# Layer A's attention: value products gathered into two runs per unit, far part of the older unit first

## The chip, the cores and the metric

The kernel runs on one core of one Trainium2 chip. The metric is the device time of one execution in microseconds, median of several runs. A core has five engines that run side by side, each through its own queue of instructions in order: TensorE (PE, matmuls, with its weight loads as PEld), VectorE (DVE), ScalarE (ACT), GpSimd (POOL) and SyncE (SP, which only issues DMAs here). They wait for each other by semaphores. Matmuls write to PSUM; the other engines move results from there to SBUF.

## The reference

A decoder trunk of two layers over 1024 tokens of width 1024 in float32. Layer A is a sparse attention of 16 heads in 4 groups, with three branches that a sigmoid gate weighs (scores on compressed blocks of keys; 8 chosen of 16 blocks of 64 keys for each query and group; the last 256 keys), and a SwiGLU. Layer B attends over shared keys in three dilations. The change is in layer A's attention:

```
def nsa_attention(h, w_in, b_gate, ...):
    ...
    p, denom, _ = masked_softmax(s + bias_c, dist_c >= 0)
    p_cmp = p / jnp.maximum(denom, 1e-30)
    o_cmp = jnp.einsum('bgrsn,bngd->bsgrd', p_cmp, v_cmp.astype(jnp.float32))
    ...
    _, sel_idx = lax.top_k(score, top_n)
    ...
        p_sel, den, _ = masked_softmax(s_sel, (dist >= 0)[:, :, :, None, :])
        return jnp.einsum('bcgrk,bgckd->bcgrd', p_sel / jnp.maximum(den, 1e-30), vg.astype(jnp.float32))
    ...
    o_win, _ = banded_attention(q, kvh(kwn), kvh(vwn), WIN - 1, 1, rel_bias)
    g = jax.nn.sigmoid((gl + b_gate).astype(jnp.float32)).reshape(B, S, N_KV, GQA_R, 3)
    o = g[..., 0:1] * o_cmp + g[..., 1:2] * o_sel + g[..., 2:3] * o_win
```

## The kernel before

Layer A's attention goes over 32 units: for each of 4 groups of heads (g) 8 tiles of 128 queries (t). A unit has 4 heads. All its weights, already divided by their sums and multiplied by the gate, lie in SBUF with the queries on the partitions, so they must be turned (transposed) before they can be multiplied with the values.

A unit's steps, as letters of the table `steps`: `a` and `b` are near scores (L821; the keys of the last 256 tokens in blocks t-2 to t, together with the 63 compressed blocks) of heads 0, 1 and 2, 3; `c` are the weights of the compressed blocks and, for t of 4 and more, the choice of key blocks; `m` turns that choice into rows of the queries (L876); `f` and `g` are far scores (L908, L909; the selected branch over all t + 1 blocks of keys) of the two pairs of heads; `n` are near values, `v` far values (both L436). A score tile `s` in PSUM (4 buffers) is read by a reduction on DVE (L822, L824, L910) that adds the bias and finds the extreme; then come ACT (L801, exponentials with sums), DVE (L803, reciprocals) and POOL (L805, scaling).

For values, `turned` (L367) takes one block of 128 keys: four transposes on PE (L371) into a PSUM tile `pt` (3 buffers), and one copy (L378) into an SBUF tile `pT` (5 buffers), in turn on ACT and DVE. `values` (L417) makes parts of up to three blocks: the transposes of a part, and then its products with the values (L436). A block's products are two matmuls of 64 columns each, for the heads of the upper and the lower half of the output; the float32 matmul appears as two records each in the profile, so a block has four. Near values have one part, of 1 to 3 blocks and the turned compressed weights (`vc`); far values have one part for 1 to 3 blocks, two for 4 to 6 and three for 7 and 8. Near and far of a unit add up in the same half of the PSUM tile `o`, near first; two units in turn use the two halves. A copy on DVE (L923) takes the finished half to `oT`.

`turn(i)` (L958) records the steps of neighbouring units in one order: near scores `a` of unit i+2; `m` and `f` of unit i; far values `v` of unit i-1; `b` and `c` of unit i+2; `n` and `g` of unit i. Loads for later units are issued at a turn's head by SyncE, the near keys (`load_kw`) three units ahead. The written order is not the last word: a scheduler places the instructions of each engine when the program is built, within their dependences and the `after` marks, which keep an instruction behind another.

Of the kernel before, what the change touches and what calls it, by code (L numbers as in the profile page):

```python
# [129 lines left out]
def trunk(ctx, tc, I, out):  # L130
# [85 lines left out]
    def after(prev):  # L216
        return tc.issue_after(prev.ins) if prev is not None else ExitStack()
# [173 lines left out]
    copies, pt_bufs = [0], [5]  # L391
# [25 lines left out]
    def values(p, po, Ps, vs, first, last, behind=None, more=None):  # L417

        nb = len(vs)
        ends = [nb * (i + 1) // -(-nb // 3) for i in range(-(-nb // 3))]
        for lo, hi in zip([0] + ends, ends):
            ts = []
            for b in range(lo, hi):
                copies[0] += 1
                t, prev = turned(p, [Ps[hp][:, e, b * 128:(b + 1) * 128] for e in range(2) for hp in range(2)],
                                 (nc.scalar.copy, nc.vector.tensor_copy)[copies[0] % 2])
                ts.append(t)
            ops = [(vs[b], vs[b], ts[b - lo][:, :256], ts[b - lo][:, 256:]) for b in reversed(range(lo, hi))]  # L430
            if more is not None and lo == 0:
                ops.append(more)
            for i, (*v, ta, tb) in enumerate(ops):
                with after(prev), after(behind if lo == i == 0 else None):
                    for e, t in enumerate((ta, tb)):
                        mm = nc.tensor.matmul(po[64 * e:64 * e + 64, :256], v[e], t, start=first and lo == i == 0,  # L436
                                              stop=last and hi == nb and i == len(ops) - 1, skip_group_check=True)
                prev = mm
        return prev
# [34 lines left out]
    with ExitStack() as c:  # L474
# [332 lines left out]
        def near_scores(g, t, hp):  # L807
# [8 lines left out]
            for e in range(2):  # L816
# [3 lines left out]
                for z in range(2):  # L820
                    nc.tensor.matmul(ps[:, :w], q, K[z][:, :w], start=z == 0, stop=z == 1)  # L821
# [58 lines left out]
        def near_values(g, t):  # L880
            pc = blocks_[g, t][0]
            pT, _ = turned(wk, [pc[:, 2 * c:2 * c + 2, :] for c in range(2)], nc.vector.tensor_copy)
            po = po_[g, t] = outs()
            k0 = max(t - 2, 0)
            ends[0] = values(wk, po, grp["P2", g, t], [grp["V", 1, g, b // 4][:, b % 4, :] for b in range(k0, t + 1)],
                             True, False, ends[0], (vc[:, g, :64], vc[:, g, 64:], pT[:, :256], pT[:, :256]))

        def far_scores(g, t, hp):
# [10 lines left out]
            for e in range(2):  # L899
                hh = 2 * hp + e  # L900
                q = query(g, t, hh)
                for i, (lo, hi, a) in enumerate(cuts):
# [6 lines left out]
                    nc.tensor.matmul(ps[:, :max(rw, 256)], ql[:nr], kl[:nr, ks], start=False, stop=True)  # L909
# [9 lines left out]
        def far_values(g, t):  # L919
            po = po_[g, t]  # L920
            ends[0] = values(wk, po, grp["P1", g, t], [grp["V", 0, g, b // 4][:, b % 4, :] for b in range(t + 1)],
                             False, True)
            nc.vector.tensor_copy(oT[:, 2 * g:2 * g + 2, tok(t)], po.rearrange("p (c q) -> p c q", q=128))  # L923
# [50 lines left out]
    with ExitStack() as c:  # L974
# [10 lines left out]
        outs, ends = Turns([o_[:, :256], o_[:, 256:]]), [None]  # L985
        for i in range(0, len(units) + 1):
            turn(i)
    kctx.close()
# [1137 lines left out]
```

## Time and profile before

| | us |
|---|---|
| median of 3 runs | 2747.96 (2747.43 to 2748.98) |
| the profiled execution | 2750.92 |
| its span, first to last instruction | 2749.1 |
| layer A's attention, first to last value product | 283.3 to 671.8 |
| mean granted TensorE clock, share of full | 0.999 |

In the answers of the profile, a row names an instruction by its line, engine, operation and its tiles, output first (`o<-pT,V`: value products of turned weights with far values; `VW` are near values, `vc` the compressed ones). `L436` is line 436 of the kernel before. For a matmul, the first size is that of the stationary operand, the second that of the moving one (128\*64 and 128x256: a contraction over 128 keys, 64 columns of the array, 256 columns of queries). The ends of matmuls are modelled and overlap, so the distance between two starts tells more about TensorE than the busy time.

### The profile page before, as it was taken

How to read it: one execution, taken by the hardware profiler on the slowest of the kernel's cores; microseconds unless marked ns; L12 is line 12 of the kernel's file. 1: busy time of each engine (PE TensorE's matmuls, PEld its weight loads, DVE VectorE, ACT ScalarE, POOL GpSimd, SP SyncE). 2: the span in 40 equal slices, each digit the busy share in tenths (PEclk: the TensorE clock that was granted, in tenths of full speed). 3: DMA queues.
4: the chain of work that ended last, by engine and by line, in shares of the span. 5: the costliest groups of instructions: out<-in, count | busy, mean ns of one | idle time of the engine just before them, and what ended most of it. 6: DMA issues, size and time to landing. Idle time of an engine off the chain costs nothing.

```text
span 2749.1 us, 42939 instructions
## 1 busy us (share of the span) xinstructions
PE 2714.2 (99%) x14448; PEld 2212.3 (80%) x14448; DVE 2211.1 (80%) x4532; ACT 1409.9 (51%) x3165; POOL 1372.5 (50%) x1446
## 2 busy tenths in 40 slices
PE   9999999999999999999999999999999999999999
PEld 8988676776888888888878888888878888888887
DVE  5443888986988989898885677688899888898888
ACT  5531777775653334344454544577766433343435
POOL 3135655552356656556356787411103755656562
PEclk9999999999999999999999999999999999999999
DMA  5678743223122232222223555697441212112112
GB/s 173 188 235 299 202 126 107 63 74 143 54 73 62 73 82 66 69 58 74 65 89 115 144 149 172 208 268 237 113 176 45 75 56 60 50 52 64 54 54 77
DMA packets 291900, 312.24 MB, mean 114 GB/s; under 512 B 50300, under 2 KB 229165, under 8 KB 291680
## 3 DMA queue, kind: packets, MB, share of 16 engines
q1 hardware_dynamic: 271280, 247.30, 30.6%
q0 software_dynamic: 20400, 62.20, 7.3%
q8 instruction: 114, 1.87, 0.3%
q14 instruction: 106, 0.87, 0.1%
HBM read 241.99 MB, written 81.04 MB: 118 GB/s over the span
## 4 chain that ended last, share of the span: by engine, by line
PE 88%; DVE 5%; DMA 3%; ACT 1%; SPq 1%; issue 1%; POOL 0%; ACTq 0%; DVEq 0%; POOLq 0%
PE ux L1241 19%; PE uy L1241 16%; PE dx L1052 8%; PE pt L371 6%; PE dr L1052 6%; PE dr L1241 5%; PE o L436 4%; PE mm L239 3%; PE mm L240 3%; PE mm L241 3%; PE o L412 2%; PE dx L1241 2%; PE s L821 1%; DVE pl L1011 1%; PE s L909 1%; PE dx L239 1%
## 5 line engine op out<-in xcount | busy, mean ns | idle before, releaser
L1011 DVE TENSOR_TENSOR pl<-oT,ph 128x512 fp32r<-128x512 f32 x336 | 343.4, 1040 | 74.1 <-PE ux L1241 19.5
L1010 ACT ACTIVATE ph<-oT 128x512 fp32r<-128x512 f32 x342 | 209.7, 627 | 232.7 <-PE ux L1241 54.6
L371 PE MATMUL pt<-ident,P 128*128 128x128 f32 x1536 | 232.2, 278 | 2.9 <-ACT pT L378 1.3
L1011 DVE TENSOR_TENSOR pl<-oTb,ph 128x512 fp32r<-128x512 f32 x228 | 207.9, 935 | 24.0 <-PE dr L1052 17.2
L1010 ACT ACTIVATE ph<-oTb 128x512 fp32r<-128x512 f32 x234 | 142.6, 626 | 161.8 <-PE ux L1241 53.4
L1446 POOL TENSOR_TENSOR oT<-oT,gffn 128x512 f32<-128x512 f32 x92 | 115.7, 1268 | 216.9 <-DMA oT<-in_ffn_w_up_dram 92.6
L371 PEld LDWEIGHTS pt<-ident,P 128*128 128x128 f32 x1536 | 174.9, 141 | 59.9 <-issue 42.9
L805 POOL TENSOR_SCALAR P<-P,sm,gates 128x384 f32<-128x384 f32 (+7 forms) x256 | 182.1, 722 | 81.6 <-DVE sm L803 57.6
L1057 DVE TENSOR_TENSOR xrfx<-xrfx,dr 128x512 f32<-128x512 f32 x320 | 204.0, 678 | 13.6 <-PE dr L1052 13.6
L1057 DVE TENSOR_TENSOR xrfx<-xrfx,dx 128x512 f32<-128x512 f32 x320 | 204.0, 676 | 0.9 <-PE dx L1052 0.9
L801 ACT ACTIVATE P<-P,m 128x384 f32<-128x384 f32 (+7 forms) x256 | 170.6, 668 | 35.6 <-DVE m L914 13.9
L1446 POOL TENSOR_TENSOR oTb<-oTb,gffn 128x512 f32<-128x512 f32 x92 | 107.6, 1179 | 161.0 <-DMA oTb<-in_ffn_w_up_dram 98.5
L378 DVE COPY pT<-pt 128x512 f32<-128x512 f32 (+1 forms) x208 | 131.6, 644 | 36.8 <-PE pt L371 30.8
L378 ACT COPY pT<-pt 128x512 f32<-128x512 f32 x176 | 100.4, 576 | 102.9 <-PE pt L371 102.4
L1932 ACT ACTIVATE P<-P,st 128x384 f32<-128x384 f32 (+2 forms) x256 | 139.4, 547 | 24.4 <-DVE st L1927 24.1
L1927 DVE CUSTOM_DVE_ANT_0 P<-s,T 128x384 f32<-128x384 f32 (+2 forms) x256 | 110.2, 475 | 6.6 <-PE s L1957 1.6
L1052 PE MATMUL dx<-ph,pl 128*128 128x512 f32 x320 | 107.2, 390 | 0.5 <-DVE pl L1011 0.5
L1052 PE MATMUL dx<-ph 128*128 128x512 f32 x320 | 107.3, 389 | 0.0
L910 DVE CUSTOM_DVE_ANT_0 P<-s,T 128x128 f32<-128x128 f32 (+3 forms) x192 | 99.2, 549 | 7.2 <-PE s L909 6.9
L239 PE MATMUL mm<-hH,wh 128*128 128x512 f32 (+1 forms) x272 | 102.8, 379 | 0.0
L240 PE MATMUL mm<-hL,wh 128*128 128x512 f32 (+1 forms) x272 | 102.6, 379 | 0.0
L241 PE MATMUL mm<-hH,wl 128*128 128x512 f32 (+1 forms) x272 | 102.3, 377 | 0.0
(649 smaller groups left out, 8028.5 us busy)
## 6 DMA issues: line engine op xcount, KB each, us to landing
qB<-xrfx POOLq DMA_DIRECT2D x96, 256.0 KB, 5.1
oT<-in_ffn_w_up_dram SPq DMA_DIRECT2D x92, 256.0 KB, 2.9
oTb<-in_ffn_w_up_dram SPq DMA_DIRECT2D x92, 256.0 KB, 2.9
Q<-qB SPq DMA_DIRECT2D x40, 512.0 KB, 6.9
wd<-in_ffn_w_down_dram SPq DMA_DIRECT2D x60, 256.0 KB, 2.6
oT<-in_b_w_q_dram SPq DMA_DIRECT2D x48, 256.0 KB, 3.5
wraw<-in_a_w_in_dram SPq DMA_DIRECT2D x18, 512.0 KB, 5.7
KW<-kS SPq DMA_DIRECT2D x96, 96.0 KB, 2.7
```

Of the source, the lines that this page charges most:

```text
L239: nc.tensor.matmul(ps, lh, rh, start=first, stop=False, skip_group_check=bool(shared))
L240: nc.tensor.matmul(ps, lh, rl, start=False, stop=False, skip_group_check=bool(shared))
L241: return nc.tensor.matmul(ps, ll, rh, start=False, stop=last, skip_group_check=bool(shared))
L371: prev = nc.tensor.transpose(ps[:, i * 128:(i + 1) * 128], h, ident)
L378: copy(t[:, :w], ps[:, :w])
L805: nc.gpsimd.tensor_scalar(P[:, e, :n], P[:, e, :n], sm[:, e:e + 1], gate(e), op0=OP.mult, op1=OP.mult)
L1010: self.high = nc.scalar.activation(h, src, AF.Copy)
L1011: self.last = (eng or nc.vector).tensor_sub(l, src, f32(h))
L1052: nc.tensor.matmul(banks[t], part(a, t)[u], b[v], start=z == 0 and onX != 2, stop=z == 2, skip_group_check=True)
L1057: nc.vector.tensor_add(xs, xs, banks[t])
L1241: mm = nc.tensor.matmul(b, x[:, i * 128:(i + 1) * 128], ys[i], start=first and (z, i) == (0, 0), stop=(z, i) == (2, 3), skip_group_check=True)
L1446: nc.gpsimd.tensor_mul(v, v, gains[:, k:k + 4].unsqueeze(2).to_broadcast([128, 4, 128]))
```

## The change

The value products are no longer made at the end of each part. `values` is replaced by `values_parts`, which only turns the blocks of a part, holds them in a list (`held`) and returns one function per part, and `held_values`, which makes the products of all that is held in one run. Within a run the far part of the older unit, whose half of `o` is already opened, comes first, with the part turned last ahead; then the near part of the newer unit opens the other half. Each run is kept behind the last run, behind the last transposes that were held, and behind the last score matmul recorded (`scored`).

In `turn(i)`, units of three far parts (t of 6 and 7) have a first run in mid-turn with their first two parts. The remaining far part or parts of unit i-1 are turned behind the near blocks of unit i, and both have one run at the turn's end. Units with two far parts have the first of them turned in mid-turn, and held. Scores stand between the turned parts: `m` and `f` of unit i first, the first far part of unit i-1, then `a` of unit i+2, the second far part (where there are three), and `b`, `c`, `g`. The copy of a finished half to `oT` is recorded with the next part that is turned, not at once. There are 12 `pT` buffers instead of 5, and the program sets the space for POOL's DMA descriptors to 4096 bytes of a partition.

```diff
-    copies, pt_bufs = [0], [5]
+    copies, pt_bufs = [0], [12]
...
-    def values(p, po, Ps, vs, first, last, behind=None, more=None):
...
+    held, opened, ended, outputs, scored = [], set(), [None], [], [None]
+
+    def values_parts(p, po, Ps, vs, more=None, done=None):
+
+        def part(lo, hi):
+            ops = [more()] if more is not None and lo == 0 else []
             for b in range(lo, hi):
                 copies[0] += 1
                 t, prev = turned(p, [Ps[hp][:, e, b * 128:(b + 1) * 128] for e in range(2) for hp in range(2)],
                                  (nc.scalar.copy, nc.vector.tensor_copy)[copies[0] % 2])
...
+                ops.append((vs[b], vs[b], t[:, :256], t[:, 256:]))
+            held.append((po, ops, done if hi == len(vs) else None, prev))
+            while outputs:
+                outputs.pop(0)()
...
+    def held_values():
+
+        prev = held[-1][3]
+        run = [h for h in reversed(held) if id(h[0]) in opened] + [h for h in held if id(h[0]) not in opened]
+        over = [id(h[0]) for h in run if h[2] is not None]
+        last = {id(h[0]): k for k, h in enumerate(run)}
+        for k, (po, ops, done, _) in enumerate(run):
+            u = id(po)
+            for i, (*v, ta, tb) in enumerate(reversed(ops)):
+                with after(prev), after(ended[0]), after(scored[0]):
                     for e, t in enumerate((ta, tb)):
...
+                opened.add(u)
                 prev = mm
...
+        ended[0] = prev
+        held.clear()
...
-            for what, d in [('a', 2), ('m', 0), ('f', 0), ('v', -1), ('b', 2), ('c', 2), ('n', 0), ('g', 0)]:
-                if 0 <= i + d < len(units):
-                    steps[what](units[i + d])
+            far = steps['v'](units[i - 1]) if i > 0 else []
...
+            some([('m', 0), ('f', 0)])
+            if len(far) == 3:
+                far.pop(0)()
+            some([('a', 2)])
+            if len(far) == 2:
+                far.pop(0)()
+                if len(held) == 2:
+                    held_values()
+            some([('b', 2), ('c', 2), ('g', 0)])
+            for part in (steps['n'](units[i]) if 0 <= i < len(units) else []) + far:
+                part()
+            if held:
+                held_values()
...
-    nc = bacc.Bacc("TRN2", target_bir_lowering=False, num_devices=1)
+    nc = bacc.Bacc("TRN2", target_bir_lowering=False, num_devices=1, dynamic_dma_scratch_size=4096)
```

What the scheduler made of it, in TensorE's order, at unit (1, 4), whose turn ends with the near values of its own blocks 2, 3 and 4 (`VW`, two tiles) and has the far values of unit (1, 3), four blocks (`V`). Before, the first part of the far values:

```order
L909 MATMUL s<-K_3014,QM_4332 128x512
L436 MATMUL o<-pT,V_3019 64x256 x2
L371 MATMUL pt<-ident,P_4871 128x128
L371 MATMUL pt<-ident,P_4992 128x128
L371 MATMUL pt<-ident,P_4871 128x128
L371 MATMUL pt<-ident,P_4992 128x128
L436 MATMUL o<-pT,V_3019 64x256 x2
L371 MATMUL pt<-ident,pc_2527 128x128 x2
```

and some 20 rows later, before too, the second part and then the near values:

```order
L371 MATMUL pt<-ident,P_4750 128x128
L436 MATMUL o<-pT,V_3019 64x256 x4
L876 MATMUL pt<-ident,mk 16x128
L908 MATMUL s<-K_3013,Q_4324 128x256
L908 MATMUL s<-K_3013,Q_4324 128x512
L371 MATMUL pt<-ident,P_5047 128x128
L908 MATMUL s<-K_3013,Q_4326 128x256
L908 MATMUL s<-K_3013,Q_4326 128x512
L371 MATMUL pt<-ident,P_5047 128x128
L436 MATMUL o<-pT,VW_4334 64x256 x2
L436 MATMUL o<-pT,VW_3912 64x256 x4
L436 MATMUL o<-pT,vc 64x256 x2
```

In the changed order the same products, at the end of the turn:

```order
L371 MATMUL pt<-ident,P_4929 128x128
L893 MATMUL pt<-ident,mk 16x128
L929 MATMUL s<-K_3013,Q_4323 128x256
L929 MATMUL s<-K_3013,Q_4323 128x512
L929 MATMUL s<-K_3013,Q_4325 128x256
L929 MATMUL s<-K_3013,Q_4325 128x512
L447 MATMUL o<-pT,V_3019 64x256 x2
L371 MATMUL pt<-ident,P_5026 128x128
L447 MATMUL o<-pT,V_3019 64x256 x6
L447 MATMUL o<-pT,VW_4333 64x256 x2
L447 MATMUL o<-pT,VW_3911 64x256 x4
L447 MATMUL o<-pT,vc 64x256 x2
```

Products that stood in four places stand in two, with one transpose of the next unit between them; the score matmuls that parted the far and the near products now stand ahead of all of them. In the whole stage the products have 107 places before and 48 after.

On VectorE, the copy of the finished half to `oT`. Before (the output is that of unit (1, 3)), behind a copy of a turned block:

```order
L378 COPY pT<-pt 128x512
L851 TENSOR_TENSOR dg<-cd,gates 128x4
L923 COPY oT<-o 128x2x128
L859 TENSOR_REDUCE a_5140<-pn 128x55
L803 RECIPROCAL sm<-sm 128x2
```

and in the changed order:

```order
L880 TENSOR_TENSOR sc<-sc,a_5117 128x16
L881 TENSOR_TENSOR sc<-sc,force 128x16
L883 MAX m_5124<-sc 128x8
L944 COPY oT<-o 128x2x128
L885 MATCH_REPLACE s_5126<-m_5124,sc 128x16
L931 ISA P_5223,mp<-s,T_4335 128x256
```

The copy moved behind the sums over the compressed weights (`a`, `sc`), which stood behind it before, and ahead of the reductions of the next unit's far scores.

More of the change, by code (lines that the diff above doesn't have):

```diff
@@ L428, in values @@
                                  (nc.scalar.copy, nc.vector.tensor_copy)[copies[0] % 2])
[L429 to L434, printed above, removed]
+                ops.append((vs[b], vs[b], t[:, :256], t[:, 256:]))
+            held.append((po, ops, done if hi == len(vs) else None, prev))
+            while outputs:
+                outputs.pop(0)()
+        nb = len(vs)
+        ends = [nb * (i + 1) // -(-nb // 3) for i in range(-(-nb // 3))]
+        return [lambda lo=lo, hi=hi: part(lo, hi) for lo, hi in zip([0] + ends, ends)]
+    def held_values():
[7 more added lines that the diff above has]
+                with after(prev), after(ended[0]), after(scored[0]):
                     for e, t in enumerate((ta, tb)):
-                        mm = nc.tensor.matmul(po[64 * e:64 * e + 64, :256], v[e], t, start=first and lo == i == 0,
-                                              stop=last and hi == nb and i == len(ops) - 1, skip_group_check=True)
+                        mm = nc.tensor.matmul(po[64 * e:64 * e + 64, :256], v[e], t, start=u not in opened,
+                                              stop=u in over and last[u] == k and i == len(ops) - 1,
+                                              skip_group_check=True)
+                opened.add(u)
                 prev = mm
-        return prev
+            if u in over and last[u] == k:
+                opened.discard(u)
+                outputs.extend(h[2] for h in run if h[0] is po and h[2])
+        ended[0] = prev
+        held.clear()
     def pipelined(jobs, lag=1):
@@ L820, in near_scores @@
                 for z in range(2):
[L821 removed]
+                    scored[0] = nc.tensor.matmul(ps[:, :w], q, K[z][:, :w], start=z == 0, stop=z == 1)
                 nc.vector.tensor_tensor_reduce(out=P[:, e, :n], in0=ps[:, DH:DH + n], in1=grp["TW", g, hh][:, 384 - n:],
@@ L881, in near_values, with blocks @@
             pc = blocks_[g, t][0]
-            pT, _ = turned(wk, [pc[:, 2 * c:2 * c + 2, :] for c in range(2)], nc.vector.tensor_copy)
+            def blocks():
+                pT, _ = turned(wk, [pc[:, 2 * c:2 * c + 2, :] for c in range(2)], nc.vector.tensor_copy)
+                return vc[:, g, :64], vc[:, g, 64:], pT[:, :256], pT[:, :256]
             po = po_[g, t] = outs()
             k0 = max(t - 2, 0)
-            ends[0] = values(wk, po, grp["P2", g, t], [grp["V", 1, g, b // 4][:, b % 4, :] for b in range(k0, t + 1)],
-                             True, False, ends[0], (vc[:, g, :64], vc[:, g, 64:], pT[:, :256], pT[:, :256]))
+            return values_parts(wk, po, grp["P2", g, t], [grp["V", 1, g, b // 4][:, b % 4, :] for b in range(k0, t + 1)],
+                                blocks)
         def far_scores(g, t, hp):
@@ L920, in far_values, with done @@
             po = po_[g, t]
-            ends[0] = values(wk, po, grp["P1", g, t], [grp["V", 0, g, b // 4][:, b % 4, :] for b in range(t + 1)],
-                             False, True)
-            nc.vector.tensor_copy(oT[:, 2 * g:2 * g + 2, tok(t)], po.rearrange("p (c q) -> p c q", q=128))
+            def done():
+                nc.vector.tensor_copy(oT[:, 2 * g:2 * g + 2, tok(t)], po.rearrange("p (c q) -> p c q", q=128))
+            return values_parts(wk, po, grp["P1", g, t], [grp["V", 0, g, b // 4][:, b % 4, :] for b in range(t + 1)],
+                                None, done)
         def loads(g, t):
@@ L961, in turn, with some @@
                 load_kw(i + 3)
-            for what, d in [('a', 2), ('m', 0), ('f', 0), ('v', -1), ('b', 2), ('c', 2), ('n', 0), ('g', 0)]:
-                if 0 <= i + d < len(units):
-                    steps[what](units[i + d])
+            far = steps['v'](units[i - 1]) if i > 0 else []
+            def some(order):
+                for what, d in order:
+                    if 0 <= i + d < len(units):
+                        steps[what](units[i + d])
+            some([('m', 0), ('f', 0)])
[11 more added lines that the diff above has]
+                held_values()
         proj_q(6)
@@ L984, in trunk @@
         o_ = psum["o"].tile([128, 512], F32, name="o", bufs=1)
-        outs, ends = Turns([o_[:, :256], o_[:, 256:]]), [None]
+        outs = Turns([o_[:, :256], o_[:, 256:]])
         for i in range(0, len(units) + 1):
             turn(i)
+        for f in outputs:
+            f()
     kctx.close()
```

6 lines of the change are left out of this document (1 added, 5 removed).

## The prediction, made before the changed kernel ran

> **What bounds the kernel now.** I read the page first, for the busy engine, then the stage of layer A's attention by windows, then what TensorE waits for there, and last single rows in order of time.
>
> ```profile
> PE 2714.2 (99%) x14448; PEld 2212.3 (80%) x14448; DVE 2211.1 (80%) x4532; ACT 1409.9 (51%) x3165; POOL 1372.5 (50%) x1446
> ...
> PE 88%; DVE 5%; DMA 3%; ACT 1%; SPq 1%; issue 1%; POOL 0%; ACTq 0%; DVEq 0%; POOLq 0%
> ```
>
> TensorE (PE) is busy 99% of the span and makes up 88% of the chain that ended last. The change touches one stage only; its value products begin at 283.3 us and end at 671.8 us:
>
> ```profile
> L436 PE MATMUL o<-pT,V x576: 379/379/431, 292.5 to 671.3; 128*64 128x256 f32 x192
> L436 PE MATMUL o<-pT,VW x336: 379/379/431, 283.3 to 661.8; 128*64 128x256 f32 x168
> L436 PE MATMUL o<-pT,vc x128: 379/379/379, 283.8 to 662.2; 128*64 128x256 f32 x128
> ```
>
> These 1040 records are 260 blocks of 128 keys, four records each. The stage by stretches (columns: stretch, its length, busy time of PE, PEld, DVE, ACT, POOL with counts, granted clock, DMA share and GB/s): the ramp of the first units, then the rest of group 0, and groups 1 to 3.
>
> ```profile
> 276.00:316.30 40.30, 35.13 (x204) 24.91 (x203) 31.76 (x168) 31.08 (x119) 29.78 (x64) 0.96 0.85 222
> ...
> 316.30:389.10 72.80, 71.45 (x514) 51.66 (x515) 60.15 (x264) 50.89 (x152) 39.08 (x70) 1.00 0.58 152
> 389.10:486.30 97.20, 95.95 (x672) 68.38 (x671) 80.75 (x367) 71.58 (x227) 56.05 (x101) 1.00 0.36 101
> 486.30:581.60 95.30, 93.99 (x668) 68.12 (x666) 80.28 (x368) 70.52 (x224) 53.20 (x92) 1.00 0.30 84
> 581.60:671.80 90.20, 87.18 (x620) 61.59 (x618) 69.18 (x281) 60.28 (x168) 42.44 (x63) 1.00 0.21 71
> ```
>
> After the ramp PE is busy 97 to 99% and VectorE (DVE) 77 to 84%. What PE waited for from 316.3 us on, in total, times and longest:
>
> ```profile
> PE o L436 <- ACT pT L378: 2.8, 6, 0.7
> PE pt L371 <- ACT pT L378: 1.3, 3, 0.5
> PE o L436 <- DVE pT L378: 0.9, 4, 0.3
> PE pt L371 <- DVE pT L378: 0.6, 2, 0.3
> ```
>
> These four are all but 0.2 us of it: 5.6 us in 355. So PE sets the pace, and what counts is how densely its instructions start. The busy share hides this, since matmuls overlap; starts show it (columns: start, length, then the instruction):
>
> ```profile
> 364.80 0.40 PE L909 MATMUL s<-K,QM 80*128 80x512 f32 x1
> 365.04 0.60 PE L371 MATMUL pt<-ident,P 128*128 128x128 f32 x4
> 365.57 1.08 PE L436 MATMUL o<-pT,V 128*64 128x256 f32 x8
> 366.58 1.10 PE L371 MATMUL pt<-ident,P 128*128 128x128 f32 x8
> ...
> 370.39 0.66 PE L371 MATMUL pt<-ident,P 128*128 128x128 f32 x4
> 370.88 0.38 PE L371 MATMUL pt<-ident,pc 128*128 128x128 f32 x2
> 371.02 0.36 PE L908 MATMUL s<-K,Q 128*128 128x256 f32 x1
> ...
> 477.56 0.65 PE L436 MATMUL o<-pT,V 128*64 128x256 f32 x4
> 478.14 0.66 PE L371 MATMUL pt<-ident,P 128*128 128x128 f32 x4
> ...
> 481.01 1.51 PE L436 MATMUL o<-pT,V 128*64 128x256 f32 x12
> 482.45 0.66 PE L371 MATMUL pt<-ident,P 128*128 128x128 f32 x4
> ...
> 656.43 0.38 PE L371 MATMUL pt<-ident,pc 128*128 128x128 f32 x2
> 656.65 0.60 PE L371 MATMUL pt<-ident,P 128*128 128x128 f32 x4
> ```
>
> **What a change between value products and other work costs.** Two transposes in a row start 0.22 us apart from what follows (656.43 to 656.65), so one is 0.11. One block of products takes 477.56 to 478.14, 0.58 us until the next transpose; three blocks take 481.01 to 482.45, 1.44. Two more blocks cost 0.86, so a block is 0.43 and leaving a run of products costs 0.58 - 0.43 = 0.15 us. The four transposes behind a run take 0.49 (370.39 to 370.88) where four are 0.44: 0.05 more. The four ahead of a run take 0.53 (365.04 to 365.57): 0.09 more. Together **0.30 us for each run of value products**, whatever its length. The value products use half the array's columns (128*64 in the rows) and everything around them all of them (128*128); whatever the cause, the price hangs on the changeover, and no wait is shown at these rows.
>
> **The change part by part.**
>
> *Fewer runs.* In the stage's order before, the products stand in 107 runs; as written they would be 92 (32 of near keys, 60 of far keys), and the scheduler cut some. In the changed order they stand in 48: one at the end of each of 33 turns, one more for each of the 8 units with 7 or 8 far blocks, and 7 cuts by the scheduler. Matmuls, transposes, copies and DMAs stay the same in number on every engine. 59 runs fewer x 0.30 = **17.7 us off PE's path**, if PE still sets the pace.
>
> *The ramp.* In the first 40.3 us PE is busy for only 35.1; it waits on others, and its longest waits are these:
>
> ```profile
> PE s L821 <- DVE cm L824: 1.2, 2, 0.8
> PE s L821 <- DVE sc L864: 1.2, 1, 1.2
> PE s L821 <- DMA KW<-kS: 0.6, 1, 0.6
> ```
>
> Six runs become three there; 3 x 0.30 = 0.9 us saved beside waits are worth nothing. The bound is 0 to 0.9; I take the loss of 0.9.
>
> *VectorE in the middle units.* In units 1 to 5 of a group, DVE is nearly as full as PE (groups 1 and 2, then unit 2 of group 2):
>
> ```profile
> 392.50:453.10 60.60, 59.81 (x415) 43.05 (x416) 54.65 (x249) 45.77 (x146) 35.95 (x62) 1.00 0.22 65
> 490.10:550.70 60.60, 60.15 (x420) 43.75 (x420) 55.08 (x250) 46.10 (x145) 36.17 (x63) 1.00 0.23 67
> ...
> 499.60:508.70 9.10, 9.10 (x67) 6.68 (x68) 9.03 (x44) 7.93 (x27) 5.10 (x11) 1.00 0.37 119
> ```
>
> Of the 59 runs saved, about 9 per group lie here: 8 as written (one each in units 1 and 2, two each in 3, 4 and 5) and one from fewer cuts. That is 2.8 us per group, 11.2 in all. PE's 60.6 us would become 57.8 against DVE's 54.7 to 55.1: DVE must be 95% busy instead of 91%. The last row shows that 99% is possible for 9 us without PE falling idle, but there scores, transposes and products alternated finely. Now a run of up to ten blocks lasts 4.3 us in which DVE gets no new scores. So the loss lies between 0 and 11.2 us; I take 40%, **4.5 us**, nearer to nothing because of that row.
>
> *The wait at a run's head.* Each run first reads the block turned last. Ahead of 19 of the 107 runs, and now of 16 of the 48, less than 0.7 us of PE work stands behind the turning of that block. The exposed waits are alike, so I take 0. The bounds: PE waited 3.7 us on L436 after the ramp and could lose all of that; the upper end is the slow rival below.
>
> *Moved instructions.* The copy of a finished output (L923) leaves the end of the far products and goes behind the next unit's first turned part. Its wait goes:
>
> ```profile
> DVE oT L923 <- PE o L436: 12.2, 15, 3.5
> ```
>
> DVE idled 12.2 us at the head of its queue there. Nobody on the chain waited through it, so it is worth 0 directly, but it is room that the middle units need. What is late next at that place is the copy of a turned block. The second near-key scores (L821) now come behind the first far scores, and SyncE issues 51 loads in other places; near keys are loaded three units ahead, tens of microseconds against a landing of 2.7:
>
> ```profile
> KW<-kS SPq DMA_DIRECT2D x96, 96.0 KB, 2.7
> ```
>
> I cost that at nothing; without the cover it would be one landing per unit. Seven more pT buffers cover runs that hold up to ten tiles plus the next ones; with them no transpose should wait for a run to end. The descriptor space for POOL's DMAs is set to 4096 bytes. POOL's queue is this row of the page (packets, MB, share of 16 engines):
>
> ```profile
> q0 software_dynamic: 20400, 62.20, 7.3%
> ```
>
> Among PE's waits above, in the ramp and after it, none is for a transfer of POOL's. I take 0; if room ran short, POOL's stores would be late behind POOL's idle half (50% busy), so the upper end is a few us at a handful of stores. The last unit still ends in transposes, a copy and three blocks of products: 0.
>
> *Sum.* 17.7 - 0.9 - 4.5 = 12.3 us off. The profiled execution took 2750.92 us around a span of 2749.1; less 12.3 it is 2738.6. It ran 3.0 us above the median of the runs (2747.96). On the median: **2736 us**.
>
> **A rule that speaks against it.** The longest unbroken row of transposes grows from 16 (1.99 us at 665.50, granted clock 1.00 in its stretch) to 26, some 2.9 us. One stretch of the stage, behind two PE waits, had half the clock:
>
> ```profile
> 311.30:314.70 3.40, 3.40 (x14) 2.83 (x12) 1.96 (x8) 1.78 (x4) 2.08 (x6) 0.51 1.00 180
> ```
>
> It cost about half of 3.4, 1.7 us. The Trainium skill, "TensorE: Matmul & The Clock Gate", section on PE-mode transpose, says that transposes do not count as a busy array for the clock gate in the way matmuls do. By that rule alone longer rows of transposes would bring such stretches back; by the trace, where 16 in a row left the clock alone, the sum stays (rival E has the other time).
>
> **The rivals.**
>
> A, the forecast, 56%: 2729 to 2740.
>
> B, 20%: DVE sets the pace in units 1 to 5 and all 11.2 us are lost there. Left are 17.7 - 0.9 - 11.2 = 5.6 us: 2742. For it: 91% busy. Against: the 9 us at 99%, and the 12.2 us of idle time that go.
>
> C, 13%: the change doesn't save what it says, because work comes in lumps. During a 4.3 us run DVE has at most four waiting score tiles, 4 reductions of 0.68 us (the row below), 2.7 us; it then idles 1.6 us and PE waits for it afterwards. Over 12 units (3, 4 and 5 of each group) that is 19 us, all of the gain: 2748, give or take 5.
>
> ```profile
> 368.32 0.68 DVE L910 CUSTOM_DVE_ANT_0 P<-s,T 128x512 f32<-128x512 f32 x1
> ```
>
> D, slower, 8%: every run waits at its head for the copy of the block turned last, since nothing of it may start earlier. The price per run is that of the two full waits before:
>
> ```profile
> 664.48 1.08 PE L436 MATMUL o<-pT,V 128*64 128x256 f32 x8 [0.62 <-ACT pT L378]
> ...
> 670.19 1.08 PE L436 MATMUL o<-pT,V 128*64 128x256 f32 x8 [0.67 <-ACT pT L378]
> ```
>
> 48 x 0.67 = 32 us, less the 3.7 there are now, less 17.7: 11 us slower, 2759. It decides from an average of (17.7 + 3.7)/48 = 0.45 us per run. Against it: only 16 runs stand that close.
>
> E, slower, 3%: half-clock stretches return, by the mechanism above. At one for each of the 12 units with the longest runs it is 12 x 1.7 = 20 us against 12.3 saved: 2756. Against it: a clock of 1.00 from 316 us on.
>
> **How the numbers follow.** A measurement of this kernel tells about 0.2%, 5.5 us, from no change: faster means under 2742.5. A is faster; B lies on the border, half and half; C is the same; D and E are slower. Faster 0.56 + 0.10 = 0.66, same 0.10 + 0.13 = 0.23, slower 0.11. The range leaves out D, E and a gain above 19 us (the full 17.7 and part of the waits): 2729 to 2750.
>
> **What would show it.** In the changed profile: 48 runs of o in the stage, each still 0.15 us beyond 0.43 a block; the products ending near 659 us instead of 671.8; PE's waits on copies of pT near 5 us. B shows as DVE at 95% or more with PE waiting for scores' banks in units 1 to 5; C as PE and DVE idle in turn; D as 20 us or more of waits of o on pT; E as a granted clock under 1.00. If the stage keeps its length with 48 runs, the price of a changeover was a wait in disguise and my main term is wrong.

## The result, and the profile after

| | before | after |
|---|---|---|
| median of 5 runs, us | 2747.96 (2747.43 to 2752.23) | 2768.3 (2764.41 to 2772.08) |
| the profiled execution, us | 2750.92 | 2768.3 |
| its span, us | 2749.1 | 2766.5 |
| value products of layer A, first to last start, us | 283.3 to 671.3 | 282.8 to 687.4 |

The ratio is 1.0074, with a 95% interval of 1.0062 to 1.0085: the changed kernel is slower by 20 us, 0.7%. From the first to the last value product the stage grew from 388.1 to 404.6 us; the rest of the span is 2361.0 and 2361.9 us. So 16.5 of the 17.4 us between the two profiled executions lie in the stage that was changed.

The page of the changed kernel, busy times and the chain that ended last:

```profile
PE 2717.2 (98%) x14448; PEld 2221.6 (80%) x14448; DVE 2211.1 (80%) x4532; ACT 1406.2 (51%) x3165; POOL 1385.7 (50%) x1446
...
PE 81%; DVE 10%; ACT 3%; DMA 2%; issue 2%; POOL 2%; SPq 0%; ACTq 0%; POOLq 0%; DVEq 0%
```

The counts are those of before, and so is the work of every engine within 1%. But the chain now goes through DVE for 10% of the span and through PE for 81%, where it was 5% and 88%: PE waits more. The value products by tile (L447 is L436 of before, columns as there):

```profile
L447 PE MATMUL o<-pT,V x576: 379/379/689, 293.4 to 687.4; 128*64 128x256 f32 x192
...
L447 PE MATMUL o<-pT,VW x336: 379/379/634, 282.8 to 678.0; 128*64 128x256 f32 x168
```

They end 16 us later than before, not 12 us earlier. The stage behind its ramp, as one stretch, first of the kernel before and then of the changed one, there followed by units 1 to 5 of group 1:

```profile
316.30:671.80 355.50, 348.58 (x2467) 249.75 (x2468) 290.36 (x1273) 253.28 (x768) 190.77 (x325) 1.00 0.35 99
```

```profile
316.30:687.80 371.50, 348.23 (x2443) 255.15 (x2441) 293.43 (x1267) 248.67 (x766) 189.53 (x321) 1.00 0.30 85
398.00:460.00 62.00, 57.44 (x395) 42.16 (x393) 52.53 (x239) 44.93 (x140) 36.56 (x61) 1.00 0.23 67
```

PE's busy time is the same, and its idle time went from 6.9 to 23.3 us. DVE did not fill up: it is busy 79% of the stretch (82% before), and 85% in units 1 to 5 of group 1. Both have room, and each waits for others. What PE waited for from 316.3 us to the stage's end, the first six rows:

```profile
PE o L447 <- ACT pT L378: 5.7, 8, 2.1
PE pt L371 <- POOL P L822: 4.2, 10, 1.5
PE pt L371 <- ACT pT L378: 3.5, 5, 0.9
PE s L929 <- DVE mp L931: 2.3, 10, 0.6
PE pt L893 <- DVE pT L378: 1.3, 6, 0.3
PE o L447 <- DVE pT L378: 0.7, 4, 0.2
```

And the answer to DVE's 12.2 us at the head of its queue:

```profile
DVE oT L944 <- PE o L447: 31.7, 13, 5.4
```

Four rows of before with 5.6 us have become a dozen kinds: transposes (`pt`) wait for copies and for weights, scores (`s`) for DVE, products for the copies. The copy of the finished half, which was to leave the head of DVE's queue, stands there for 31.7 us.

One turn's end shows how. PE, ACT and DVE in unit (1, 5), in order of time (start, length, instruction, and in brackets the idle time before it with what ended it):

```profile
454.93 0.66 PE L371 MATMUL pt<-ident,P 128*128 128x128 f32 x4
455.69 0.28 PE L893 MATMUL pt<-ident,mk 128*16 128x128 f32 x1
455.94 0.30 PE L371 MATMUL pt<-ident,P 128*128 128x128 f32 x1
458.38 2.81 PE L447 MATMUL o<-pT,V 128*64 128x256 f32 x24 [2.14 <-ACT pT L378]
461.02 1.47 PE L447 MATMUL o<-pT,VW 128*64 128x256 f32 x12
462.32 0.60 PE L447 MATMUL o<-pT,vc 128*64 128x256 f32 x4
462.85 1.20 PE L930 MATMUL s<-K,QM 80*128 80x512 f32 x4
```

```profile
455.70 1.04 ACT L818 ACTIVATE P<-P,m 128x896 f32<-128x896 f32 x1
...
456.74 1.03 ACT L818 ACTIVATE P<-P,m 128x896 f32<-128x896 f32 x1
...
457.76 0.57 ACT L378 COPY pT<-pt 128x512 f32<-128x512 f32 x1
```

```profile
457.89 0.17 DVE L820 RECIPROCAL sm<-sm 128x2 f32<-128x2 f32 x1 [1.07 <-ACT P L818]
462.97 0.42 DVE L944 COPY oT<-o 128x256 f32<-128x256 f32 x1 [4.91 <-PE o L447]
463.39 0.69 DVE L931 CUSTOM_DVE_ANT_0 P<-s,T 128x512 f32<-128x512 f32 x1
```

The last block's transposes are done at 456.2, but its copy stands on ACT behind two exponentials, and PE idles 2.14 us. Then ten blocks of products run for 4.47 us (458.38 to 462.85), and in that time DVE has nothing to do: it idles 4.91 us, copies the finished half, and only then reduces scores again. The run itself costs what was reckoned, 10 x 0.43 + 0.15 = 4.45. A second place shows the transposes, late in the same group:

```profile
482.93 0.87 PE L371 MATMUL pt<-ident,P 128*128 128x128 f32 x6 [0.33 <-POOL P L822]
484.11 0.55 PE L371 MATMUL pt<-ident,P 128*128 128x128 f32 x3 [0.30 <-POOL P L822]
485.28 1.09 PE L371 MATMUL pt<-ident,P 128*128 128x128 f32 x8 [0.62 <-ACT pT L378]
```

Six transposes are worth 0.66 us and three 0.33, but the next ones start 1.18 and 1.17 us later: the row of transposes stops for weights and for copies, with no products left to put in between.

### The profile page after: what moved, and what is told of

Its sections match the earlier page's. It is cut to its first block, busy times and chain, and to the rows that moved or that the text cites. A ratio compares the mean times of both kernels' runs of the same rounds, so it can differ in the third digit from the quotient of the medians.

```text
span 2766.5 us, 42934 instructions
## 1 busy us (share of the span) xinstructions
PE 2717.2 (98%) x14448; PEld 2221.6 (80%) x14448; DVE 2211.1 (80%) x4532; ACT 1406.2 (51%) x3165; POOL 1385.7 (50%) x1446
## 4 chain that ended last, share of the span: by engine, by line
PE 81%; DVE 10%; ACT 3%; DMA 2%; issue 2%; POOL 2%; SPq 0%; ACTq 0%; POOLq 0%; DVEq 0%
PE ux L1284 19%; PE uy L1284 16%; PE dx L1095 8%; PE dr L1095 6%; PE dr L1284 5%; PE pt L371 3%; PE o L447 3%; PE mm L239 2%; PE mm L240 2%; PE mm L241 2%; PE o L412 2%; DVE P L931 2%; DVE pl L1054 1%; PE dx L1284 1%; POOL P L822 1%
## 5 line engine op out<-in xcount | busy, mean ns | idle before, releaser
L1054 DVE TENSOR_TENSOR pl<-oTb,ph 128x512 fp32r<-128x512 f32 x228 | 208.1, 935 | 26.2 <-PE dr L1095 17.4
L1100 DVE TENSOR_TENSOR xrfx<-xrfx,dr 128x512 f32<-128x512 f32 x320 | 204.3, 679 | 13.0 <-PE dr L1095 12.9
```

Of the source, the lines that this page charges most:

```text
L1054: self.last = (eng or nc.vector).tensor_sub(l, src, f32(h))
L1100: nc.vector.tensor_add(xs, xs, banks[t])
```

## The experiments

Two measures are used for all kernels. The **rest** is the stage (first to last start of a value product) less 0.30 us for each run of products: all that isn't a changeover. **PE's stalls** add up, over the stage with its ramp, how much later each instruction of PE started than the prices of those ahead of it allow: 0.11 us for a transpose, 0.43 for a block of products, 0.12 to 0.23 for a score matmul by its columns, 0.30 for a run. They are larger than PE's waits in the views above, since the modelled ends of matmuls fill part of the idle time: 23 us before and 56 us after. They are estimates: with slightly other prices, and with the 0.30 us of a run divided otherwise between its two sides, a total moves by up to 4 us and one of its three parts by up to 5. Time at half the granted clock is in them too.

The theories, with letters of their own. **L**: the work comes in lumps; while transposes stand in a row, and then products, the engines behind and ahead of PE have nothing, and PE waits for them later. **L-pt** says that the three `pt` tiles of a row of transposes are its narrow place, **L-s** the four score tiles. **H**: the copy to `oT` waits at the head of DVE's queue and keeps scores from being reduced. **B**: the 12 `pT` buffers or the descriptor space cost time. **O**: the new order of the steps, not the joining, costs it.

| kernel | runs of products (longest, blocks) | stage us | rest us | PE's stalls us (pt / s / o) | median us | ratio to before, 95% |
|---|---|---|---|---|---|---|
| before | 107 (4) | 388.1 | 356.0 | 23.1 (5.8 / 10.4 / 7.0) | 2747.96 | |
| after | 48 (10) | 404.6 | 390.2 | 55.8 (22.2 / 21.6 / 12.0) | 2768.3 | 1.0074 (1.0062 to 1.0085) |
| e1_copy_behind | 48 (10) | 408.6 | 394.2 | 59.5 (22.4 / 23.9 / 13.2) | 2770.41 | 1.0074 (1.0057 to 1.0091) |
| e2_buffers_only | 107 (4) | 387.4 | 355.3 | 22.9 | 2747.74 | 0.9999 (0.9990 to 1.0008) |
| e3_order_only | 112 (4) | 384.8 | 351.2 | 18.8 (3.9 / 10.1 / 4.8) | 2748.15 | 0.9997 (0.9988 to 1.0006) |
| e4_joined_per_branch | 67 (8) | 390.2 | 370.1 | 36.3 (12.9 / 14.5 / 8.8) | 2754.46 | 1.0025 (1.0016 to 1.0035) |
| e5_pt4_s3 | 48 (10) | 387.0 | 372.6 | 40.5 (8.5 / 27.2 / 4.8) | 2751.75 | 1.0013 (1.0003 to 1.0022) |
| e6_pt2_s5 | 48 (10) | 443.6 | 429.2 | 92.7 (45.2 / 26.3 / 21.2) | 2804.75 | 1.0207 (1.0192 to 1.0222) |
| e7_more_copies_on_act | 51 (10) | 408.7 | 393.4 | 60.0 (34.9 / 11.5 / 13.6) | 2774.4 | 1.0097 (1.0082 to 1.0113) |
| e8_end_run_apart | 76 (6) | 386.5 | 363.7 | 29.6 (10.6 / 12.2 / 6.8) | 2747.5 | 0.9996 (0.9987 to 1.0005) |
| c1_before_pt4_s3 | 99 (6) | 398.7 | 369.0 | 35.8 (14.3 / 15.6 / 5.9) | 2758.61 | 1.0034 (1.0022 to 1.0046) |
| c2_end_apart_pt4_s3 | 75 (8) | 387.3 | 364.8 | 33.8 (8.6 / 19.5 / 5.7) | 2751.73 | 1.0012 (1.0003 to 1.0021) |
| c3_parts_of_four_pt4_s3 | 89 (4) | 391.4 | 364.8 | 31.8 | 2755.43 | 1.0028 (1.0017 to 1.0038) |
| c4_order_only_pt4_s3 | 99 (6) | 390.7 | 361.0 | 29.4 | 2752.52 | 1.0016 (1.0006 to 1.0025) |
| f1_parts_of_four | 82 (4) | 390.4 | 365.8 | 32.5 | 2753.46 | 1.0018 (1.0009 to 1.0027) |
| f2_order_only_far_first | 104 (4) | 392.4 | 361.2 | 28.4 | 2753.28 | 1.0020 (1.0012 to 1.0029) |

Each ratio is to the kernel before on the same chip (medians 2747.74 to 2749.68). The runs are counted in PE's order of starts, since the scheduler cuts and joins some.

### The copy of the finished half put behind the scores (theory H)

The changed kernel, with the copy to `oT` kept behind the last far reduction of the next turn:

```diff
-            while outputs:
-                outputs.pop(0)()
...
             some([('m', 0), ('f', 0)])
+            while outputs:
+                with after(reduced[0]):
+                    outputs.pop(0)()
```

> The changed kernel, but the copy of a finished half to oT stands on VectorE behind the reductions of the next far scores (32 copies moved, nothing else). Theory H (VectorE stands 31.7 us at the head of its queue before these copies, and scores and turned blocks behind it are late): those waits fall to a few us, PE's stalls of 56 us fall by up to 20, and the time comes to 2748 to 2754. Theory L (lumps: three pt tiles and four s tiles cannot cover the longer stretches of transposes and scores) and theory O (the new order of steps): VectorE's wait goes, but PE waits elsewhere; 2763 to 2772, as the changed kernel.

Measured: 2770.41 us, ratio 1.0074, as the changed kernel. DVE's longest wait, in the stage (lines of this kernel stand three lower: L928 is the reduction of far scores, L941 the copy):

```profile
DVE P L928 <- PE s L927: 27.0, 11, 6.9
...
DVE oT L941 <- PE o L444: 6.7, 4, 4.1
```

The wait at the head of the queue moved from the copy to the reduction of the next scores, with nearly its size. DVE does not hold scores back behind the copy; there are none to reduce while the products run. H falls.

### Buffers and descriptor space alone (theory B)

The kernel before, with these two lines of the change:

```diff
-    copies, pt_bufs = [0], [5]
+    copies, pt_bufs = [0], [12]
...
+    nc = bacc.Bacc("TRN2", target_bir_lowering=False, num_devices=1, dynamic_dma_scratch_size=4096)
```

> The kernel before with 12 pT buffers and the 4096 bytes for POOL's descriptors, nothing else. Theory B (space or buffers cost the time): 2755 or more. All others: 2745 to 2751, with 107 runs of products.

Measured: 2747.74 us, ratio 0.9999; stage, runs and stalls are those of before. B falls.

### The new order without the joining (theory O)

The changed kernel, but products are made after each part that was turned:

```diff
             if len(far) == 3:
                 far.pop(0)()
+                held_values()
...
-                if len(held) == 2:
-                    held_values()
+                held_values()
...
                 part()
-            if held:
                 held_values()
```

Here a unit's near products open the other half of `o` while the older unit's last far part is still to come, and earlier sums of the older unit are lost; with the two parts the other way round (f2, below) the sums are whole. The instructions are the same in number and size.

> The changed kernel's order of steps, but each part's products follow its transposes, as before: 112 runs instead of 48. At 0.30 us a run that is 19 us of changeovers more than in the changed kernel. Theory L (joining makes the lumps): PE's stalls fall from 56 to about 25 us, which pays for the changeovers: 2748 to 2758. Theory O (the order of steps is what makes PE wait): stalls stay near 56 us and the changeovers come on top: 2780 to 2790.

Measured: 2748.15 us, ratio 0.9997, 112 runs and the fewest stalls of all, 18.8 us. The new order of steps, with scores between the turned parts, costs nothing here; joining the products does. The same order with whole sums (f2) costs 5 us, so up to a quarter of the 20 us could be order. O falls as the main cause.

### One run per unit and branch, in the old order (theory L)

The kernel before with 12 buffers and the descriptor space, and parts as long as the branch:

```diff
-        ends = [nb * (i + 1) // -(-nb // 3) for i in range(-(-nb // 3))]
+        ends = [nb]
```

> The kernel before in its order of steps, but far values of a unit are turned whole and multiplied in one run: 67 runs instead of 107, the longest of 8 blocks; 12 pT buffers. 40 runs fewer are 12 us. Theory O: the stalls stay at 23 us and the time falls to about 2736. Theory L: the lumps come here too, up to 8 blocks turned at a stretch, and eat most or all of it: 2743 to 2760.

Measured: 2754.46 us, ratio 1.0025. 40 runs fewer should save 12.0 us; the rest grew by 14.1. Joining gives back what it saves in the old order too, as L expected.

### More and fewer tiles for the transposes (L-pt against L-s)

The kernel divides eight PSUM tiles in this stage: four `s`, three `pt`, one `o`. The changed kernel was run with one tile moved to either side:

```diff
-        score_bank = lambda: psum["s"].tile([128, 512], F32, name="s", bufs=4) if "s" in psum else bank(first_banks())
+        score_bank = lambda: psum["s"].tile([128, 512], F32, name="s", bufs=3) if "s" in psum else bank(first_banks())
...
+        BANKS["pt"] = 4
```

and with `bufs=5` and 2.

> The changed kernel with four pt tiles and three s tiles in PSUM instead of three and four. In all kernels so far the stage's length follows from 0.30 us a run plus PE's stalls (56 us in the changed kernel: 22 ahead of transposes, 22 ahead of scores, 12 ahead of products). L-pt (three tiles for turned blocks are the limit): stalls ahead of transposes fall by 10 or more, time 2753 to 2760. L-s (score tiles are the limit): stalls ahead of scores rise by 10 or more, 2776 to 2790. L-rate (VectorE's and ScalarE's queues set the pace in the stretches between runs, a tile more only moves the stall): within 5 us of 2768.

> The changed kernel with two pt tiles and five s tiles. L-s: stalls ahead of scores fall by 10 or more, time 2753 to 2760. L-pt: stalls ahead of transposes rise by 10 or more, 2776 to 2800. L-rate: within 5 us of 2768.

Measured: 2751.75 and 2804.75 us, beside 2768.3 with three. PE's main waits behind the ramp, with four `pt` tiles and then with two:

```profile
PE s L929 <- DVE cm L841: 3.9, 6, 0.8
PE pt L371 <- POOL P L822: 2.3, 1, 2.3
PE o L447 <- ACT pT L378: 2.0, 3, 0.8
...
PE pt L371 <- ACT pT L378: 0.5, 1, 0.5
```

```profile
PE pt L371 <- DVE pT L378: 13.6, 23, 1.5
PE o L447 <- ACT pT L378: 7.7, 14, 1.3
PE pt L371 <- POOL P L822: 6.0, 5, 2.8
PE pt L371 <- ACT pT L378: 5.4, 17, 0.7
PE o L447 <- DVE pT L378: 4.9, 7, 0.8
```

And a row of transposes with two tiles:

```profile
488.62 1.27 PE L371 MATMUL pt<-ident,P 128*128 128x128 f32 x8 [0.25 <-DVE pT L378]
490.07 1.16 PE L371 MATMUL pt<-ident,P 128*128 128x128 f32 x8 [0.17 <-DVE pT L378]
491.60 0.30 PE L371 MATMUL pt<-ident,P 128*128 128x128 f32 x1 [0.37 <-DVE pT L378]
```

Eight transposes fill two tiles and are worth 0.88 us; the next eight start 1.45 us later, and the ones after that 1.53, when a copy has freed a tile. A tile moved from `s` to `pt` made the joined kernel 17 us faster, and one moved the other way 36 us slower. Both go the way that L-pt said, a little beyond its ranges, and against L-s. With four tiles the stalls of transposes fall from 22.2 to 8.5 us, and those of scores rise from 21.6 to 27.2, as a tile of theirs is gone. (In the kernel with two, three stretches of some 6.8 us ran at half the granted clock, each at a gap in PE's work; they lose at most 10 us, where the changed kernel lost 3.4.)

The tiles are not all that changed, though. In both kernels the scheduler also placed PE's instructions anew: the longest unbroken row of transposes is 32 in the kernel with four `pt` tiles and 28 in the one with two, where the changed kernel has 26. So the 17 and the 36 us belong to the tiles and the new order together; L-pt is what both directions and the stalls speak for, and the tile by itself was not measured.

The Trainium skill, "TensorEngine Tiling (Array Packing)", section "PSUM Bottleneck", warns that after the fourfold speed of a tiled TensorE the copies out of PSUM may become what limits, and asks for both ScalarE and VectorE there. The runs agree in kind, with a difference: PE was not faster over the stage, the copies were already shared, and DVE is 79% busy and ACT 67% (248.67 of 371.50 us). By the two runs above, what ran short is most likely the place for transposes that wait for a copy.

### Two of three copies on ACT

DVE is the fuller of the two engines, so the changed kernel was run with

```diff
-                                 (nc.scalar.copy, nc.vector.tensor_copy)[copies[0] % 2])
+                                 (nc.scalar.copy, nc.vector.tensor_copy, nc.scalar.copy)[copies[0] % 3])
```

> The changed kernel with two of three copies of turned blocks on ScalarE instead of one of two: some 38 copies of 0.60 us of queue time leave VectorE (23 us), ScalarE gets 38 of 0.48 (18 us). L-rate with VectorE as the limit: PE's stalls fall by 10 to 20, time 2748 to 2759. L-rate with both engines alike, or a limit by latency (weights that come late by way of ScalarE, VectorE and POOL): 2764 to 2775.

Measured: 2774.4 us, ratio 1.0097. PE's first wait is now

```profile
PE pt L371 <- ACT pT L378: 13.2, 10, 2.3
```

Scores stall less (11.5 us instead of 21.6), as DVE has less to do, and transposes more (34.9 instead of 22.2), as more copies can stand behind ACT's exponentials, like the one in unit (1, 5). The stall goes where the copies go. The stage behind its ramp, as one stretch:

```profile
316.30:692.00 375.70, 346.20 (x2451) 257.18 (x2447) 268.14 (x1229) 265.66 (x801) 189.67 (x321) 0.98 0.31 84
```

DVE is busy 71% of it instead of 79%, and no time came of that, which speaks against DVE's rate as the limit. That the kernel is slower than the changed one is not shown to come of the copies: with its ramp the stage had 17 us at half the granted clock, which lose at most 8.5 us where the changed kernel lost 3.4, and it is only 4.1 us longer (408.7 against 404.6).

### The last run cut in two

The changed kernel, with the far parts turned and multiplied at the turn's end, and then the near parts turned and multiplied:

```diff
-            for part in (steps['n'](units[i]) if 0 <= i < len(units) else []) + far:
-                part()
-            if held:
-                held_values()
+            for parts in (far, steps['n'](units[i]) if 0 <= i < len(units) else []):
+                for part in parts:
+                    part()
+                if held:
+                    held_values()
```

> The changed kernel, but at a turn's end the far part is turned and multiplied first, then the near part by itself: 76 runs, the longest of 6 blocks, 28 changeovers (8.4 us) more than in the changed kernel. L (longer runs make the stalls): stalls lie midway, near 38 us, time near 2759 (2754 to 2763). If run length has nothing to do with it, the stalls stay at 56 and the time is 2777.

Measured: 2747.5 us, ratio 0.9996. Two rows, of DVE's waits in the stage and of the same unit (1, 5):

```profile
DVE oT L944 <- PE o L447: 3.3, 6, 1.2
```

```profile
450.04 1.52 PE L447 MATMUL o<-pT,VW 128*64 128x256 f32 x12 [0.17 <-ACT pT L378]
```

Where the joined run waited 2.14 us for a copy, the near products wait 0.17, and DVE's 31.7 us behind `o` are 3.3. Undoing one join gives the whole loss back, more than was expected (the stalls are 29.6 us and not near 38); 31 runs fewer than before save 9.3 us and the rest costs 7.7.

### A fourth tile where little is joined

The same two lines (`pt` 4, `s` 3) in the kernel before, in e8, and in the two kernels of the next section:

> The kernel before with four pt tiles and three s tiles (99 runs as the scheduler now cuts them). If the fourth pt tile helps because runs are long, it does little here: 2743 to 2752. If three pt tiles held every order back alike, this kernel gains as the changed one did (16 us): 2729 to 2736.

> Far and near runs apart at a turn's end, with four pt tiles and three s tiles: 75 runs. Theory L-pt: the stalls left ahead of transposes (11 us) shrink, those ahead of scores grow somewhat; 2738 to 2746, better than both kernels. If the two remedies are one and the same (either takes the stalls away, the second adds only the lack of a score tile): 2747 to 2755.

> The kernel before in its order, but parts of up to four blocks instead of three, seven pT buffers, four pt tiles and three s tiles: 89 runs, no run over four blocks. 18 runs fewer are 5.4 us. Theory L-pt: runs no longer than before cost no more stalls, 2740 to 2746. If the score tile that is missing costs more than that: 2748 or more.

> The changed order of steps, products behind each part as before, a turn's far part ahead of its near part, four pt tiles and three s tiles: 99 runs. Beside the order-only kernel with three pt tiles (2748) it shows whether the fourth tile helps where runs are short: by theory L-pt within 5 us of 2748; if it helps every order, 2732 to 2740.

Measured, by the medians: 11 us slower than before, 4 slower than e8, 2 slower than f1, 1 less than f2. So the fourth tile, at the price of a score tile and with the scheduler's new order, is worth 17 us to the joined kernel and nothing or less to the others. Not all of this is as L-pt had it: c2 is not better than both its parents, which is the reading that the two remedies are one, c3 is slower than the 2740 to 2746 of L-pt, and c1 lies above both of its ranges. In c1 the scheduler placed instructions anew (99 runs, the longest of 6 blocks), and PE stands three times for weights:

```profile
PE pt L371 <- POOL P L805: 8.0, 3, 3.2
```

Its stage also lost up to 6.8 us at half the granted clock, where the kernel before lost 1.7. Most of its 11 us is thus these waits and the clock; what the missing score tile costs was not separated.

### Small steps: parts of up to four, and the new order with whole sums

The kernel before with `-(-nb // 4)` for `-(-nb // 3)` and 7 buffers (f1); and e3 with the far parts ahead of the near ones at the turn's end, so that all sums are whole (f2):

```diff
-            for part in (steps['n'](units[i]) if 0 <= i < len(units) else []) + far:
+            for part in far + (steps['n'](units[i]) if 0 <= i < len(units) else []):
```

> The kernel before in its order, parts of up to four blocks instead of three, seven pT buffers, three pt and four s tiles: 82 runs instead of 107. If the price of 0.30 us a run is real and stretches of this length still fit three pt tiles: 25 x 0.30 = 7.5 us off, 2739 to 2744. If every saved run is given back as stalls: 2746 to 2752.

> The changed order of steps with products behind each part, a turn's far part ahead of its near part: 104 runs. If the order of steps alone costs nothing: 2744 to 2751, as the order-only kernel measured. If that kernel's time hung on its near part being ahead: 2755 or more.

Measured: 2753.46 and 2753.28 us, both 0.2% slower and both outside the ranges that were set. In f1, 25 runs fewer save 7.5 us and the rest grows by 9.8; its PE waits lead with weights that are late:

```profile
PE pt L371 <- POOL P L805: 4.5, 3, 2.3
PE s L909 <- ACT QM L877: 2.4, 2, 1.3
PE pt L371 <- ACT pT L378: 2.0, 5, 0.6
```

f2 against e3 is an order of two parts, and differs by 5 us. So much can a mere order move in this stage, and kernels that lie closer than that don't tell theories apart.

## Why the prediction was wrong

**The price of a run held; that PE sets the pace did not.** The 48 runs came as counted, and one of ten blocks takes 4.47 us by the price of 4.45. The prediction said that a stage of unchanged length would show its price to be a wait in disguise. It is none: leaving a run takes 0.15 to 0.17 us beyond 0.43 a block at all 107 runs before and at 45 of the 48 after, and the least found in four transposes is 0.09 ahead of a run, and 0.05 behind one where more transposes follow, in both kernels. So some 17.7 us less of changeovers stand in the changed kernel, and the stage still grew: the rest rose by 34.2. The Trainium skill, "TensorEngine Tiling (Array Packing)", section "Key Properties", says that a change of the tiling mode drains TensorE; a price at each change between products of 64 columns and full-width work fits that, though no run here separates a drain from another cause.

**The step that failed: "VectorE in the middle units".** It bounded the loss there by the saving itself, "between 0 and 11.2 us", and took 4.5. That holds if DVE is only one more engine that must keep up at its own rate. But DVE was not full (85% in units 1 to 5 of group 1 instead of the 95% reckoned), and the loss was larger than what was to be saved. A joined run ties engines together: during a 4.3 us run DVE has no new scores, and between two runs up to ten blocks are transposed (5.2 on average, where it was 2.3) with only scores among them, through three tiles that ACT and DVE must empty between their other work. (Unbroken rows of transposes grew less, from 5.1 to 5.5 transposes on average; what went is the products between them.) Nothing holds waits of that kind below the saving. The stalls show where they are: transposes 5.8 to 22.2 us, scores 10.4 to 21.6, products 7.0 to 12.0, 32.7 us together of the 34.2. The largest of the three, that of the transposes, is a term that the prediction put at nothing.

**"With them no transpose should wait for a run to end"** was true of the `pT` buffers (no copy of a turned block waits for products in the changed kernel, and by e2 the buffers cost nothing) and looked at the wrong tile. The three `pt` tiles were never priced, although the prediction's rows of before, from 364.80 us on, show the cover that the change took away: a score, four transposes, two blocks of products, eight transposes. While those products ran, DVE reduced two score tiles, and its next copy began at 366.55, as they ended: PE had work while that copy was still to come. With two, three and four tiles the joined kernel takes 2805, 2768 and 2752 us.

**"The wait at a run's head ... I take 0"**: 5 us by the stalls (the waits of products in the view rose from 3.7 to 6.4 us). Fewer runs wait longer each, where the copy turned last stands behind ACT's exponentials: the longest is 2.1 us where it was 0.7.

**Moved instructions, buffers, descriptor space, the end and the ramp**: right at about nothing (e1, e2, and the constant time outside the stage), though the ramp's 0.9 us was not measured by itself. The reading of DVE's 12.2 us was wrong: they were to go, and became 31.7, because the wait was not for a badly placed copy but for want of other work.

**The rivals.** B showed as not so: DVE is at 79% in the stage and 85% in the middle units of group 1. C was the right mechanism, "PE and DVE idle in turn", with its chance of 13% and its 19 us too small: it reckoned the score tiles alone, over 12 units, and left out the tiles of the transposes. D fell: 6.4 us of such waits, not 20 or more. E fell as the main cause: the two stretches of half clock in the stage lie near its start:

```profile
309.80:313.20 3.40, 3.04 (x14) 2.23 (x16) 3.29 (x12) 1.26 (x4) 3.37 (x6) 0.50 1.01 339
326.90:330.30 3.40, 3.40 (x20) 1.94 (x18) 2.00 (x8) 1.76 (x5) 2.99 (x5) 0.50 0.90 218
```

That is one more than before, about 1.7 us, and behind 330.3 us there is none, the longest row of transposes (26, from 678.77 us) included. Over its five runs the changed kernel's time goes with the mean granted clock, from 2764.4 us at 0.999 to 2772.1 at 0.996; the kernel before took 2748.6 by the median of the 65 runs at 0.999 beside the experiments. So at the same clock some 16 us of the loss are left.

**What stays open.** How the 34 us divide between transposes, scores and the order that the scheduler chose: the three come together in each kernel, and an order alone moved 5 us (f2 against e3). A rival to L-pt was not tested: in e4, f1 and e8 the runs saved 12.0, 7.5 and 9.3 us and the rest grew by 14.1, 9.8 and 7.7, nearly the same, so another limit may lie just behind PE. Weights that come late by way of ACT, DVE and POOL would be one, as f1's first wait shows; no run made that way shorter. What four `pt` tiles would give beside four score tiles wasn't tried, as the kernel's eight PSUM tiles are all given out. No kernel here is faster than the one before; e2, e8 and e3 (without whole sums) equal it.

## What to carry to other kernels

Work that alternates finely on TensorE paid a price at each change here, but each kind of work was the time in which other engines served the next one; before joining runs, count the PSUM tiles that the work left in a row must go through, and what the engine behind them does meanwhile. A saving counted on the busiest engine is no bound for the loss. If a run must grow, give the row ahead of it its buffers first and see who loses them: here the fourth tile, with the order that came with it, recovered 17 us, and the scores whose tile it was stalled some 3 to 6 us more.

## What was unexpected in the hardware

Idle time in PE's rows understated how late PE was: behind the ramp the waits of before are 5.6 us, while its starts are 23 us behind the prices of the rows with the ramp, and some 13 us without it. Here starts were the better measure.

Some small instructions of DVE take far longer than others of the same line. One from the order of time of the changed kernel, and one line's instructions (shortest, median and longest in ns):

```profile
444.60 1.63 DVE L880 TENSOR_TENSOR sc<-sc,a 128x16 f32<-128x16 f32 x1
...
L863 DVE TENSOR_SCALAR cd<-cd x32: 142/162/1006, 272.1 to 643.1; 128x4 f32<-128x4 f32 x32
```

The 128x4 scalar operation has a median of 0.16 us and a longest of 1.01, and the 128x16 one stands there with 1.63. The trace shows what they stand behind. The longest of L863, and POOL's work at that time:

```profile
481.89 1.01 DVE L863 TENSOR_SCALAR cd<-cd 128x4 f32<-128x4 f32 x1
...
481.67 2.38 POOL L822 TENSOR_SCALAR P<-P,sm,gates 128x1024 f32<-128x1024 f32 x2
```

The first of POOL's two instructions is over at 482.87, and DVE's at 482.90. The same holds for all twelve of the 32 that took 0.25 us or more: each ends 23 to 39 ns behind the end of an instruction on POOL. So these wait for POOL, as far as one trace tells; no run tested it.
